# A decoder block with expert gathers: token mixers in three groups of blocks instead of two

## The chip, the cores and the metric

The kernel runs on one core of a Trainium2 chip. The metric is the device time of one execution in microseconds (us). The inputs are float32 and lie in HBM; the output goes there too. "Faster" means a lower time.

## What is computed

One layer of a decoder for 1024 tokens of width 1024. The tokens form eight blocks of 128.

```python
h = rms_norm(x, norm_mix_g)
proj = h @ w_in                    # queries, keys, values of two attentions, indexer, gates
o_a = diff_attention(...)          # 4 heads, causal, two softmaxes subtracted
o_b = dsa_attention(...)           # 8 heads, each query sees its 256 best keys by the indexer
x = x + (g[:d] * (o_a @ w_branch_a) + g[d:] * (o_b @ w_branch_b)) @ w_out
x = x + memory_attention(rms_norm(x), rms_norm(mem), w_mem_q, w_mem_kv, w_mem_o)
x = x + peer_ffn(rms_norm(x), peer_w_q, peer_sub_keys, peer_u, peer_v)
return rms_norm(x, final_norm_g)

def peer_ffn(h):                   # per token 8 heads x 16 experts of 16384
    s_top, i_top = top_k(q . sub_keys, 16)       # two lists of 16 for each head
    best, idx = top 16 of the 256 pair sums; g = softmax(best)
    a = gelu(sum(h * u[idx])) * g
    return sum(a * v[idx])
```

Attention is causal: block b looks at the keys of blocks 0 to b, so blocks can be worked in groups from the front.

## The kernel before

**Groups.** `run` (L1304) goes over `GROUPS`: blocks 0 to 3, then 4 to 7. For a group it calls `phase_P` (norm, projections with w_in, the indexer's scores), `phase_T` (the two attentions, L634), `phase_G` (gates and branch products), `phase_O` (w_out), `queries_M` and `phase_M` (memory attention), `phase_R` (scores of the expert keys, written to DRAM as `pq`). Every phase streams its weights from HBM again for each group, in 256 KB tiles two to a load (`wstream`, L165). Where `WHOLE` does not name the phase and group, ScalarE and VectorE split a tile into a rounded part and a rest (L106, L107), and a product is three matmuls (L129 to L131). Where it does, one float32 matmul is used (L127). `by_pairs` takes w_out and w_mem_o of the first group for two blocks at a time.

**Experts.** Blocks 0 to 3 get their experts by gathers. After the first group `run` adds two lanes to a pace-maker. `routes` finds the 128 experts of each token of a block (`route`: a load `so<-pq`, then lists of the 16 best on VectorE, L928 to L932). `experts` gathers the rows in the fixed order `ORDER`, U then V of block 0, of block 1, and so on: 128 gathers of u rows a block (L1036, issued by GpSimd, 512 KB each), each followed by a multiply-and-sum on VectorE (L1039), and 128 gathers of v rows (L1052), each followed by a multiply-and-add (L1058); 1024 in all. Seven buffers `rows` hold gathered rows. Blocks 4 to 7 get theirs in `dense`: all 16384 experts go through TensorE and are weighted by a sparse table, which is built on chip beside the first 48 of 128 expert tiles ("early", their gelu is kept in DRAM as `ga` and read back as `c`). The rest of the tiles follow, with the second product added up in `accu` (L1282).

**What sets the order.** Each phase tells the pace-maker how much TensorE work it has emitted (`tick`, in nominal us). A lane emits its next piece when its credit allows: a gather each `u_each` nominal us, taken from `U_EACH`. A list scheduler then fixes each engine's order, with the lanes at a lower priority (`ROUTE_LAG`, `EXPERT_LAG`). On the chip each engine works its list in order. The lane `fill` puts gate products and memory keys between the attention's small matmuls, `select` the search for the 256 best keys.

```python
self.pace.add("routes", routes, ROUTE_EACH, ROUTE_LAG)
self.pace.add("experts", self.experts(routes), None, EXPERT_LAG)
```

Of the kernel before, what the change touches and what calls it, by code (L numbers as in the profile page):

```python
# [20 lines left out]
P = 128  # L21
S = 1024
D = 1024
NB = S // P
GROUPS = [[0, 1, 2, 3], [4, 5, 6, 7]]
NG = 4
ND = NB - NG
DT = ND * P
# [50 lines left out]
class K:  # L79
# [245 lines left out]
    def phase_P(self, g, st, hp, hT):  # L325
# [3 lines left out]
        with ExitStack() as ctx:  # L329
            E = ctx.enter_context  # L330
            self.pp = pp = E(self.pool("pp"))
            self.wp = E(self.pool("wP"))
            self.scr2 = (pp, "x", "h", X_BUFS[g], D)
            gm = self.gain(pp, a["norm_mix_g"], "gmix")
            for i, b in enumerate(blks):
                x = pp.tile([P, D], F32, name="x", bufs=X_BUFS[g])
                nc.sync.dma_start(x, a["x"][0, b * P:(b + 1) * P])
                h = pp.tile([P, D], F32, name="h", bufs=X_BUFS[g])
                self.norm(h, x, gm)
# [136 lines left out]
            project([(w_in, C_DSQ, 512)], 512, use_dsq)  # L476
            self.pace.tick(START_T[g])

# [155 lines left out]
    def phase_T(self, g, oT, hT):  # L634
# [3 lines left out]
        with ExitStack() as ctx:  # L638
# [1 line left out]
            SM, NR, LD = nk * P, ROWS_T[g], LOADS_T[g]  # L640
            self.scr2 = (tp, "row", "row", NR, SM)
            if g:
                self.u_each = U_EACH[g + 1]

            for h in range(4):
                ks = tp.tile([P, 2, SM], F32R, name="k", bufs=LD)
# [544 lines left out]
    def dense(self, psum, early):  # L1191
# [5 lines left out]
        with ExitStack() as ctx:  # L1197
# [19 lines left out]
            ga = {}  # L1217
            with ExitStack() as c2:
                self.wb = c2.enter_context(self.pool("wb"))
                self.u_each = U_EACH[-2]  # L1220
                self.pace.add("weights", self.weights(blks))
                for e in range(early):
                    o = first(e)
                    t = self.wb.tile([P, 512], F32, name="gelu", bufs=2)
                    nc.scalar.activation(t, o, AF.Gelu)
                    ga[e] = self.scratch([P, 512], f"ga{e}")
                    nc.sync.dma_start(ga[e], t)
                self.pace.drain("weights")
# [3 lines left out]
            for n in range(KEEP):  # L1232
                i, d = n % ND, n // ND
                kept[i, d] = self.ps.tile([P, 512], F32, name=f"kept{n}", bufs=1)
            self.u_each = U_EACH[-1]
            sp = E(self.pool("sp"))
            accu = sp.tile([P, ND, D], F32, name="accu")
            G = 4
# [65 lines left out]
    def run(self, ctx):  # L1304
# [13 lines left out]
        self.scored = set()  # L1318
        for g, self.blks in enumerate(GROUPS):
            self.GB, self.GT = len(self.blks), len(self.blks) * P  # L1320
            if g:
                self.u_each = U_EACH[g]
            psum.close()
            with self.pool(f"hT{g}", side="right") as hp, self.pool(f"W{g}", side="right") as st, \
                    self.pool(f"fp{g}", side="right") as self.fp, self.pool(f"fill{g}", side="right", space=PSUM) as self.fps:
# [10 lines left out]
            psum = self.psum_phase(psum, f"psG{g}", 6)  # L1336
            last = g == len(GROUPS) - 1
            side = "right" if last else None
# [30 lines left out]
            if g == 0:  # L1369
                self.setup_peer(ctx.enter_context(self.pool("peer", side="right")))  # L1370
                self.route_ctx = ExitStack()
                self.setup_route(self.route_ctx.enter_context(self.pool("rt", side="right")))
                self.rs, self.routed = {b: {} for b in range(NG)}, set()
                routes = self.routes(range(NG))
                self.u_each = U_EACH[0]
                self.pace.add("routes", routes, ROUTE_EACH, ROUTE_LAG)
                self.pace.add("experts", self.experts(routes), None, EXPERT_LAG)
        self.pace.drain("routes")
# [6 lines left out]
EARLY = 48  # L1385
V_AHEAD, V_EACH = 0, None
ORDER = [("U", 0), ("V", 0), ("U", 1), ("V", 1), ("U", 2), ("V", 2), ("U", 3), ("V", 3)]
ROWS_T, LOADS_T, FILL_EACH, FILL_LAG = (5, 4), (2, 2), (0.7, 2.4), 100
H_BUFS, D_BUFS, R_BUFS = (4, 2), 4, 7
X_BUFS = (3, 1)  # L1390
START_T = (0.0, 0.0)
WHOLE = {("P", 1), ("G", 1), ("M", 1)}
PAIRS = {(2, 0)}
KEEP, A_BUFS, O_BUFS = 4, 2, 2
U_BUFS, V_BUFS = 3, (4, 4, 4)
SELECT_EACH = (5.0, 7.0)
U_EACH, ROUTE_EACH = (1.9, 1.8, 1.9, 1.3, 2.0), 3.0
ROUTE_LAG, EXPERT_LAG = 300, 3000
_INS = ["x", "mem", "positions", "norm_mix_g", "w_in", "da_lambda", "da_subln_g", "w_branch_a", "w_branch_b", "gate_bias",
        "w_out", "norm_mem_g", "mem_kv_norm_g", "w_mem_q", "w_mem_kv", "w_mem_o", "norm_ffn_g", "peer_w_q",  # L1400
# [29 lines left out]
```

## Time and profile before

| What | Value |
|---|---|
| median of 3 runs | 3506.3 us (3505.97 to 3508.13) |
| the profiled execution, its span | 3509.34 us, 3507.6 us |
| TensorE (PE) busy | 3015.4 us, 86% |
| VectorE (DVE) busy | 2878.4 us, 82% |
| ScalarE (ACT), GpSimd (POOL) busy | 1396.7 us, 1380.4 us |
| moved by DMA | 964.65 MB, 275 GB/s in the mean |
| mean granted TensorE clock | 0.928 |

The span is one execution from its first to its last instruction, on the profiler's clock; the execution's own time is 1.7 us more. Busy times are unions of an engine's instructions. They are averages over stages that differ much, so they are read stage by stage. The granted clock is a share of 2.4 GHz; TensorE runs at 2.4 or at 1.2.

### The profile page before, as it was taken

How to read it: one execution, taken by the hardware profiler on the slowest of the kernel's cores; microseconds unless marked ns; L12 is line 12 of the kernel's file. 1: busy time of each engine (PE TensorE's matmuls, PEld its weight loads, DVE VectorE, ACT ScalarE, POOL GpSimd, SP SyncE). 2: the span in 40 equal slices, each digit the busy share in tenths (PEclk: the TensorE clock that was granted, in tenths of full speed). 3: DMA queues.
4: the chain of work that ended last, by engine and by line, in shares of the span. 5: the costliest groups of instructions: out<-in, count | busy, mean ns of one | idle time of the engine just before them, and what ended most of it. 6: DMA issues, size and time to landing. Idle time of an engine off the chain costs nothing.

```text
span 3507.6 us, 42342 instructions
## 1 busy us (share of the span) xinstructions
PE 3015.4 (86%) x13234; PEld 2285.7 (65%) x13234; DVE 2878.4 (82%) x6695; ACT 1396.7 (40%) x2537; POOL 1380.4 (39%) x1122
## 2 busy tenths in 40 slices
PE   8999888798787698686989995588899999999995
PEld 7777766553355575455767774466687788777884
DVE  6656544599888879888988988687799999999998
ACT  5755344245565441322546456222222222222221
POOL 0000000011235246553131466333466665767665
PEclk9999998999898799888999998799899999999998
DMA  4575443436789579897485899999999999999997
GB/s 138 162 186 133 162 140 137 132 121 198 223 259 312 139 272 356 306 328 272 163 314 189 309 379 341 375 309 321 318 351 372 376 380 365 382 379 373 383 382 265
DMA packets 394210, 964.65 MB, mean 275 GB/s; under 512 B 36712, under 2 KB 146048, under 8 KB 392576
## 3 DMA queue, kind: packets, MB, share of 16 engines
q0 software_dynamic: 155264, 560.01, 45.0%
q1 hardware_dynamic: 238720, 401.94, 33.3%
q8 instruction: 104, 1.70, 0.2%
q14 instruction: 122, 1.00, 0.1%
HBM read 871.64 MB, written 90.18 MB: 274 GB/s over the span
## 4 chain that ended last, share of the span: by engine, by line
PE 35%; DVE 21%; DMA 17%; issue 15%; POOL 8%; ACT 4%; SPq 1%; POOLq 0%; ACTq 0%; DVEq 0%
POOL rows L1036 5%; PE acc L129 5%; PE acc L131 5%; PE acc L130 5%; DMA c<-ga 4%; DVE h3s L1058 3%; DMA rows<-in_peer_v_dram,ii 2%; DMA so<-pq 2%; PE fill L127 2%; POOL rows L1052 2%; PE po L720 2%; DVE rows L1039 2%; DMA fraw<-in_w_in_dram 1%; DMA rows<-in_peer_u_dram,ii 1%; PE tps L601 1%
## 5 line engine op out<-in xcount | busy, mean ns | idle before, releaser
L1036 POOL DMA_INDIRECT rows<-in_peer_u_dram,ii x512 | 656.8, 1283 | 917.2 <-DVE rows L1039 304.9
L1052 POOL DMA_INDIRECT rows<-in_peer_v_dram,ii x512 | 660.6, 1290 | 447.4 <-DVE h3s L1058 290.9
L1058 DVE SCALAR_TENSOR_TENSOR h3s<-rows,wexp,h3s 128x1024 f32<-128x1024 f32 x508 | 651.1, 1282 | 34.4 <-DMA rows<-in_peer_v_dram,ii 25.1
L1039 DVE SCALAR_TENSOR_TENSOR rows<-rows,h3s 128x1024 f32<-128x1024 f32 x512 | 612.0, 1220 | 62.7 <-DMA rows<-in_peer_u_dram,ii 62.2
L129 PE MATMUL acc<-fT,uT 128*128 128x512 f32 x1024 | 415.6, 406 | 38.6 <-ACT uT L106 23.2
L131 PE MATMUL acc<-fT,uT 128*128 128x512 f32 x1024 | 411.8, 402 | 15.3 <-DVE uT L107 15.2
L130 PE MATMUL acc<-fT,uT 128*128 128x512 f32 x1024 | 410.5, 401 | 0.0
L106 ACT ACTIVATE c<-wl 128x512 fp32r<-128x512 f32 x128 | 80.2, 631 | 805.6 <-PE out L130 479.2
L143 POOL TENSOR_TENSOR rstd<-msq,mhalf 128x1 f32<-128x1 f32 (+1 forms) x42 | 34.0, 808 | 596.1 <-DVE msq L141 572.5
L129 PEld LDWEIGHTS acc<-fT,uT 128*128 128x128 f32 x1024 | 196.5, 192 | 84.7 <-ACT uT L106 23.6
L131 PEld LDWEIGHTS acc<-fT,uT 128*128 128x128 f32 x1024 | 196.7, 192 | 64.4 <-DVE uT L107 23.7
L106 ACT ACTIVATE uT<-uraw 128x1024 fp32r<-128x1024 f32 x128 | 135.6, 1059 | 254.2 <-PE acc L130 131.0
L130 PE MATMUL kept<-v,c 128*128 128x512 f32 x512 | 206.2, 405 | 32.3 <-DVE v L107 32.2
L129 PE MATMUL kept<-v,c 128*128 128x512 f32 x512 | 201.4, 400 | 37.1 <-ACT v L106 35.8
L130 PEld LDWEIGHTS acc<-fT,uT 128*128 128x128 f32 x1024 | 197.0, 192 | 45.3 <-issue 6.0
L129 PE MATMUL out<-v,c 128*128 128x512 f32 x512 | 203.6, 398 | 15.2 <-DVE accu L1282 15.2
L107 DVE TENSOR_TENSOR w<-wraw,w 128x512 fp32r<-128x512 f32 (+1 forms) x176 | 116.4, 680 | 116.3 <-ACT w L106 109.5
L131 PE MATMUL kept<-v,c 128*128 128x512 f32 x512 | 203.7, 398 | 0.0
L130 PE MATMUL out<-v,c 128*128 128x512 f32 x512 | 201.9, 394 | 0.0
L131 PE MATMUL out<-v,c 128*128 128x512 f32 x512 | 201.8, 394 | 0.0
L562 ACT ACTIVATE junk<-W,xb 128x384 bf16<-128x384 f32 (+5 forms) x186 | 163.7, 880 | 78.8 <-DVE xb L560 76.1
L127 PE MATMUL acc<-wraw,hT 128*128 128x512 f32 (+1 forms) x384 | 169.3, 597 | 16.2 <-ACT tok L349 7.6
(367 smaller groups left out, 6731.6 us busy)
## 6 DMA issues: line engine op xcount, KB each, us to landing
uraw<-in_peer_ut_dram SPq DMA_DIRECT2D x128, 512.0 KB, 9.2
vraw<-in_peer_v_dram SPq DMA_DIRECT2D x128, 512.0 KB, 8.8
Wd<-wbuf SPq DMA_DIRECT2D x64, 512.0 KB, 8.6
wl<-Wd SPq DMA_DIRECT2D x64, 512.0 KB, 8.4
wraw<-in_w_in_dram SPq DMA_DIRECT2D x40, 512.0 KB, 3.6
fraw<-in_w_in_dram SPq DMA_DIRECT2D x32, 512.0 KB, 6.0
wraw<-in_w_out_dram SPq DMA_DIRECT2D x24, 512.0 KB, 4.2
ga<-gelu SPq DMA_DIRECT2D x48, 256.0 KB, 5.4
```

The source lines that it names most:

```text
L106: self.nc.scalar.activation(hi, src, AF.Copy)
L107: self.last_dve = self.nc.vector.tensor_tensor(lo, src, hi.bitcast(F32), op=OP.subtract).ins
L127: self.last_pe = nc.tensor.matmul(out, l[0], r[0], start=start, stop=stop).ins
L129: nc.tensor.matmul(out, l[0], r[0], start=start, stop=False)
L130: nc.tensor.matmul(out, l[0], r[1], start=False, stop=False)
L131: self.last_pe = nc.tensor.matmul(out, l[1], r[0], start=False, stop=stop).ins
L562: nc.scalar.activation(junk[:, :(b + 1) * P], self.W[b], AF.Sign, bias=xb[:, j:j + 1].bitcast(F32), accum_out=s[:, j:j + 1])
L720: nc.tensor.matmul(po[:, h * 64:(h + 1) * 64], pT[:, j * P:(j + 1) * P], self.dsv[:, k0 + j, gg * 64:(gg + 1) * 64], start=(k0 + j == 0), ...
L1036: nc.gpsimd.indirect_dma_start(out=u, out_offset=None, in_=a["peer_u"][0], in_offset=bass.IndirectOffsetOnAxis(ap=ii[:, j:j + 1], axis=0))
L1039: nc.vector.scalar_tensor_tensor(u, u, 1.0, h3, op0=OP.mult, op1=OP.mult, accum_out=aa[:, j:j + 1])
L1052: nc.gpsimd.indirect_dma_start(out=v, out_offset=None, in_=a["peer_v"][0], in_offset=bass.IndirectOffsetOnAxis(ap=r["ii"][:, j:j + 1], axi ...
L1058: nc.vector.scalar_tensor_tensor(o, v, w[:, j:j + 1], o, op0=OP.mult, op1=OP.add)
```

## The change

Blocks 0 to 3 are mixed in two groups of two. The lanes for routing and gathers are started after the first group, as before, so the routing of blocks 0 and 1 can begin after those two blocks, and that of 2 and 3 after the second group. The last group is as it was. The tables by group have a third entry. `phase_P` makes indexer queries only for groups that have a block of 2 or more (it did so before too), so the first group of two makes none.

```diff
-GROUPS = [[0, 1, 2, 3], [4, 5, 6, 7]]
+GROUPS = [[0, 1], [2, 3], [4, 5, 6, 7]]
...
-                self.u_each = U_EACH[g + 1]
+                self.u_each = U_EACH["T", g]
...
-                self.u_each = U_EACH[-2]
+                self.u_each = U_EACH["W"]
...
-            self.u_each = U_EACH[-1]
+            self.u_each = U_EACH["D"]
...
-                self.u_each = U_EACH[g]
+                self.u_each = U_EACH["P", g]
...
-                self.u_each = U_EACH[0]
...
-ROWS_T, LOADS_T, FILL_EACH, FILL_LAG = (5, 4), (2, 2), (0.7, 2.4), 100
-H_BUFS, D_BUFS, R_BUFS = (4, 2), 4, 7
-X_BUFS = (3, 1)
-WHOLE = {("P", 1), ("G", 1), ("M", 1)}
-PAIRS = {(2, 0)}
+ROWS_T, LOADS_T, FILL_EACH, FILL_LAG = (5, 5, 4), (2, 2, 2), (0.22, 0.7, 2.4), 100
+H_BUFS, D_BUFS, R_BUFS = (2, 2, 2), 4, 7
+X_BUFS = (2, 2, 1)
+WHOLE = {("P", 2), ("G", 2), ("M", 2)}
+PAIRS = {(2, 0), (2, 1)}
...
-SELECT_EACH = (5.0, 7.0)
-U_EACH, ROUTE_EACH = (1.9, 1.8, 1.9, 1.3, 2.0), 3.0
+SELECT_EACH = (0.0, 2.5, 7.0)
+U_EACH = {("P", 1): 1.9, ("T", 1): 1.9, ("P", 2): 1.8, ("T", 2): 1.9, "W": 1.3, "D": 2.0}
+ROUTE_EACH = 3.0
```

The intervals of the gathers are the same numbers as before at the stages that were there before: 1.9 beside the mixers, 1.3 in the early experts, 2.0 in the dense ones.

**Where gathers now stand on GpSimd (POOL).** `L1036` and `L1052` are the gathers of u and v rows, `L616` and `L648` the loads of queries and keys for an attention head, `L143` a norm's root, `L907` the set-up of routing. Before, from there to the second head of the second group:

```order
L907 IOTA place 128x50
L143 TENSOR_TENSOR rstd<-msq,mhalf 128x1 x4
L1036 DMA rows<-in_peer_u_dram,ii 128x1024 x40
L616 DMA q<-daq_7439 64x4x512 x2
L648 DMA k<-dak 128x2x1024
```

In the change, from there to the third head of the second group, which now holds blocks 2 and 3:

```order
L907 IOTA place 128x50
L143 TENSOR_TENSOR rstd<-msq,mhalf 128x1 x6
L1036 DMA rows<-in_peer_u_dram,ii 128x1024 x3
L616 DMA q<-daq_4755 64x4x256 x2
L648 DMA k<-dak 128x2x512
L616 DMA q<-daq_4755 64x4x256 x2
L648 DMA k<-dak 128x2x512
L1036 DMA rows<-in_peer_u_dram,ii 128x1024
L616 DMA q<-daq_4755 64x4x256 x2
L648 DMA k<-dak 128x2x512
L1036 DMA rows<-in_peer_u_dram,ii 128x1024 x6
```

And on the same engine from that group's last attention head to the third group's first work there (`L553`, the set-up of its selection):

```order
L143 TENSOR_TENSOR rstd<-msq,mhalf 128x2
L1036 DMA rows<-in_peer_u_dram,ii 128x1024 x61
L143 TENSOR_TENSOR rstd<-msq,mhalf 128x1 x2
L1036 DMA rows<-in_peer_u_dram,ii 128x1024 x33
L143 TENSOR_TENSOR rstd<-msq,mhalf 128x1 x2
L1036 DMA rows<-in_peer_u_dram,ii 128x1024 x12
L553 IOTA flip 128x4
```

So 116 gathers (3, 1, 6, 61, 33 and 12) stand between the end of the first group and the third; none stood before the group of blocks 4 to 7.

**At the start of the early experts**, on POOL too; `L1103` is the first instruction of `make_codes`. Before:

```order
L143 TENSOR_TENSOR rstd<-msq,mhalf 128x1
L1036 DMA rows<-in_peer_u_dram,ii 128x1024
L143 TENSOR_TENSOR rstd<-msq,mhalf 128x1
L1036 DMA rows<-in_peer_u_dram,ii 128x1024 x35
L1103 IOTA ah 112x128
```

In the change:

```order
L1036 DMA rows<-in_peer_u_dram,ii 128x1024 x33
L1052 DMA rows<-in_peer_v_dram,ii 128x1024
L143 TENSOR_TENSOR rstd<-msq,mhalf 128x1 x4
L1052 DMA rows<-in_peer_v_dram,ii 128x1024 x29
L1103 IOTA ah 112x128
```

Added up from the start, 297 gathers stand ahead of it before (u of blocks 0 and 41 of block 1, v of block 0) and 414 in the change (u and v of block 0, u and 30 v of block 1).

**The last gathers on VectorE (DVE)**, among the accumulations `L1282`; `L1071` and `L148` are a block's last sum and norm. Before, the end of the program:

```order
L141 TENSOR_SCALAR msq<-ss 128x1
L1058 SCALAR_TENSOR_TENSOR h3s<-rows,wexp,h3s 128x1024 x2
L148 SCALAR_TENSOR_TENSOR uraw<-uraw,rstd,vraw 128x1024
L1058 SCALAR_TENSOR_TENSOR h3s<-rows,wexp,h3s 128x1024 x5
L1071 TENSOR_TENSOR rows<-rows,h3s 128x1024
```

In the change 20 of the 124 accumulations stand behind these rows:

```order
L107 TENSOR_TENSOR uT_29095<-uraw,uT_29094 128x1024
L1058 SCALAR_TENSOR_TENSOR h3s<-rows,wexp,h3s 128x1024
L1071 TENSOR_TENSOR rows<-rows,h3s 128x1024
L1282 TENSOR_TENSOR accu<-accu,out 128x512
L141 TENSOR_SCALAR msq<-ss 128x1
L148 SCALAR_TENSOR_TENSOR rows<-rows,rstd 128x1024
```

The last gather moved from the end of the program to a place with several groups of expert tiles behind it. In VectorE's order 481 gathers are used before the first accumulation before, 580 in the change.

## Rows read from the trace of the kernel before

**Rows 1.** Windows by stage: stretch, its length, busy us (instructions), granted clock, DMA share, GB/s.

```profile
core 0: us, PE busy (x) PEld busy (x) DVE busy (x) ACT busy (x) POOL busy (x), PEclk, DMA share, GB/s
0.00:653.00 653.00, 582.94 (x2758) 463.68 (x2758) 347.53 (x964) 331.02 (x754) 28.39 (x51) 0.95 0.51 150
653.00:1635.00 982.00, 775.45 (x2980) 491.49 (x2980) 858.81 (x2752) 426.10 (x957) 390.76 (x338) 0.88 0.74 249
1635.00:2214.00 579.00, 495.31 (x2552) 388.28 (x2552) 514.70 (x1557) 308.61 (x392) 222.21 (x172) 0.94 0.77 283
2214.00:2520.00 306.00, 235.04 (x922) 184.04 (x923) 231.00 (x295) 67.45 (x89) 109.28 (x91) 0.88 0.94 326
2520.00:3471.00 951.00, 926.68 (x4023) 758.21 (x4022) 904.17 (x1110) 260.11 (x339) 619.47 (x464) 0.99 0.99 369
3471.00:3508.00 37.00, 0.00 (x0) 0.00 (x0) 22.17 (x21) 3.45 (x6) 10.27 (x8) 0.54 0.59 199
```

**Rows 2.** Chain of waits (start, us, what): first work of two stages.

```profile
653.09 6.64 DMA x<-in_x_dram
...
1634.79 2.29 DVE codes L1114
```

**Rows 3.** Windows: the last part of the first group.

```profile
410.00:653.00 243.00, 203.86 (x824) 155.58 (x822) 102.24 (x207) 93.76 (x180) 5.06 (x11) 0.90 0.43 143
```

**Rows 4.** Groups of DVE by form, 0 to 653 us: busy us, mean ns, idle before.

```profile
L107 DVE TENSOR_TENSOR w<-wraw,w 128x512 fp32r<-128x512 f32 x128 | 85.5, 689 | 110.5 <-ACT w L106 104.1 <-PE acc L130 6.2
L107 DVE TENSOR_TENSOR f<-fraw,f 128x512 fp32r<-128x512 f32 x48 | 33.0, 688 | 37.4 <-ACT f L106 30.9 <-PE tps L355 5.1 <-PE fill L131 0.8
```

**Rows 5.** Groups of DVE by form, 650 to 1640 us: gathers, lists of 16, pair match.

```profile
L1039 DVE SCALAR_TENSOR_TENSOR rows<-rows,h3s 128x1024 f32<-128x1024 f32 x164 | 198.1, 1219 | 17.7 <-DMA rows<-in_peer_u_dram,ii 17.5
L1058 DVE SCALAR_TENSOR_TENSOR h3s<-rows,wexp,h3s 128x1024 f32<-128x1024 f32 x127 | 162.8, 1282 | 8.9 <-DMA rows<-in_peer_v_dram,ii 6.0
...
L929 DVE FIND_INDEX8 i<-v,so 128x8 uint32<-128x128 f32 x79 | 22.3, 284 | 0.0
L932 DVE FIND_INDEX8 i<-v,t 128x8 uint32<-128x128 f32 x76 | 21.5, 284 | 0.0
L931 DVE MAX8 v<-t 128x8 f32<-128x128 f32 x77 | 21.2, 282 | 0.1
L930 DVE MATCH_REPLACE8 t<-v,so 128x128 f32<-128x128 f32 x77 | 21.1, 275 | 0.0
L928 DVE MAX8 v<-so 128x8 f32<-128x128 f32 x79 | 20.7, 281 | 45.1 <-DMA so<-pq 45.1
...
L995 DVE TENSOR_TENSOR eq<-eq,kn 128x512 f32<-128x512 f32 x16 | 10.9, 680 | 0.0
```

**Rows 6.** Timeline of PE: 256-column matmuls of split products (start, length).

```profile
311.54 0.28 PE L131 MATMUL fill<-memT,f 128*128 128x256 f32 x1
311.66 0.28 PE L129 MATMUL fill<-memT,f 128*128 128x256 f32 x1
```

**Rows 7.** Windows: the dense stage beside u gathers (first) and v gathers (second).

```profile
2600.00:2700.00 100.00, 95.45 (x410) 77.24 (x409) 93.38 (x146) 26.78 (x35) 68.35 (x50) 0.98 1.00 376
2750.00:2950.00 200.00, 200.00 (x884) 165.62 (x883) 197.41 (x191) 54.02 (x70) 134.91 (x100) 1.00 1.01 379
```

**Rows 8.** The tile `ga`: its reloads (first and last start), who waited (us, times).

```profile
L1249 SPq DMA_DIRECT2D c<-ga x48: 319/323/5063, 2214.3 to 2537.2; - x48
...
DVE wl L1253: 54.0, 31
```

**Rows 9.** The tile `so`: who waited for it, and its DMAs' time to landing.

```profile
DVE v L928: 55.5, 9
...
DMA to landing us min/median/max: 2.0/3.3/16.0
```

**Rows 10.** Windows: 50 us of the second group with little TensorE work.

```profile
1150.00:1200.00 50.00, 22.20 (x128) 20.01 (x129) 46.87 (x117) 14.94 (x50) 7.74 (x8) 0.63 0.26 83
```

**Rows 11.** Timeline of DVE: the end.

```profile
3492.75 6.56 DVE L1058 SCALAR_TENSOR_TENSOR h3s<-rows,wexp,h3s 128x1024 f32<-128x1024 f32 x5
```

More of the change, by code (lines that the diff above doesn't have):

```diff
@@ L1387 @@
 ORDER = [("U", 0), ("V", 0), ("U", 1), ("V", 1), ("U", 2), ("V", 2), ("U", 3), ("V", 3)]
-ROWS_T, LOADS_T, FILL_EACH, FILL_LAG = (5, 4), (2, 2), (0.7, 2.4), 100
-H_BUFS, D_BUFS, R_BUFS = (4, 2), 4, 7
-X_BUFS = (3, 1)
-START_T = (0.0, 0.0)
-WHOLE = {("P", 1), ("G", 1), ("M", 1)}
-PAIRS = {(2, 0)}
+ROWS_T, LOADS_T, FILL_EACH, FILL_LAG = (5, 5, 4), (2, 2, 2), (0.22, 0.7, 2.4), 100
+H_BUFS, D_BUFS, R_BUFS = (2, 2, 2), 4, 7
+X_BUFS = (2, 2, 1)
+START_T = (0.0, 0.0, 0.0)
+WHOLE = {("P", 2), ("G", 2), ("M", 2)}
+PAIRS = {(2, 0), (2, 1)}
 KEEP, A_BUFS, O_BUFS = 4, 2, 2
 U_BUFS, V_BUFS = 3, (4, 4, 4)
-SELECT_EACH = (5.0, 7.0)
-U_EACH, ROUTE_EACH = (1.9, 1.8, 1.9, 1.3, 2.0), 3.0
+SELECT_EACH = (0.0, 2.5, 7.0)
+U_EACH = {("P", 1): 1.9, ("T", 1): 1.9, ("P", 2): 1.8, ("T", 2): 1.9, "W": 1.3, "D": 2.0}
+ROUTE_EACH = 3.0
 ROUTE_LAG, EXPERT_LAG = 300, 3000
```

## Prediction

> **What bounds the kernel now.** I read the windows by stage first, cut where the chain of waits and the first reload of a gelu tile show the next stage's first work [rows 1, 2, 8]: the first group 0 to 653 us, the second 653 to 1635, the early experts 1635 to 2214, the dense experts 2214 to 3471, and 37 us of final norms without a matmul. The reader should see a different limit in each.
> The first group is TensorE's: busy 583 of 653 us, while VectorE works 348 and no gather runs. Its 70 idle us fall unevenly: 39 of them lie in its last 243 us, where the output projection, memory attention and routing scores start one after another [rows 1, 3]. The second group is VectorE's: 859 of 982 us, 87%, TensorE 775. The early stage is both (515 and 495 of 579). In the dense stage after 2520 TensorE is busy 927 of 951, with VectorE at 904 and DMA at 0.99. Before 2520 it is idle 71 of 306; there VectorE waits 54 us for the reload of 48 gelu tiles, which no gather causes [rows 8].
> So 1024 gathers, each 1.2 to 1.3 us of VectorE [rows 5], start late, and VectorE idles 305 us in the first group. That is the room the change goes for.
>
> **The change, part by part.** Stages are compared with the profiled execution (3509.3 us for a span of 3507.6; the median of the runs is 3 us lower).
>
> *Matmul count.* Where the group's tokens are the moving side, a 512-column matmul becomes two of 256. By the built program's counts 288 such matmuls become 576 for each of the three products of a split multiply: 864 pairs. Undisturbed 256-column matmuls start 0.12 us apart [rows 6], 512-column ones 200/884 = 0.226 [rows 7]; a pair costs 0.24 for 0.226, some 10 us in all. Against it stand 48 matmuls (11 us) of indexer queries that blocks 0 and 1 do not need and no longer make. TensorE's work is unchanged: about 291 us for each small group.
> The Trainium skill says otherwise in TensorE: Matmul & The Clock Gate, section Back-to-back issue gap: sustained spacing is set by weight load and matmul together, 81 ns at 128 columns and 131 at 512. A straight line between them is 98 ns at 256 by estimate, so a pair would cost 65 ns more than one, 56 us over the 864. This trace shows another spacing for these split fp32 products, at both widths, and the sum goes by the trace.
>
> *First group, now blocks 0 and 1.* 291 us of matmuls, plus 4 for half of the pairs' cost, less 11. The 39 us of starts come once per group whatever its size, because each is a norm, a transpose and a first weight load in series. Of the other 31 idle us I count 22, between half and all. Sum 345. Its bounds: 323 (no idle time but the starts) and 370 (weights twice as fast per matmul and late). VectorE is no limit: 144 weight splits at 0.69 us [rows 4] and half of the rest come to 210.
>
> *Second group, blocks 2 and 3.* New here is that VectorE gets everything at once. Splits: 136 of 0.69 us and 8 narrower ones at two thirds, 98 us, since each group splits every weight again. The rest of the first group's VectorE work is 348 - 119 = 229 us [rows 1, 4]; blocks 2 and 3 carry all indexing and selection, so 120. Routing of blocks 0 and 1: a list of the 16 best costs 1.41 us over five rows and a block has 16 such lists, 23 us; the pair match has twelve steps of 0.68 a block, another 8 [rows 5], the many short steps about 14 by estimate: 45 a block, 90. Gathers: the order puts 116 before the third group's first POOL work, 140 us at 1.21. Sum 448 against 291 of TensorE. At the 87% of the present second group this takes 512 us; at 95% 472, at 80%, which 256 KB weight tiles going DMA, ScalarE, VectorE, TensorE in turn may bring, 560. I take 512, since the same mixture ran at 87%. The two small groups together: 857, or 204 more than the 653 now.
> TensorE's granted clock is a cost that hides here: where it was busy 22 of 50 us the clock was 0.63 in the mean, a mixture of 2.4 and 1.2 GHz [rows 10]. Even at 0.8 its 291 us become 364, below VectorE's 448.
>
> *Third group, the old second.* Two routings fewer (90 us of VectorE), 298 gathers for 297. VectorE 770; at 87% that is 880, a gain of 102. With TensorE at 775 of work the stage cannot follow VectorE all the way down: none to 102, and I take 70, two thirds, since VectorE's share there is 87% and TensorE's 79%. Eight loads of scores fewer, at up to 16 us each [rows 9], are inside this.
>
> *Early experts.* 166 gathers for 184, same interval 1.3: 23 us of VectorE between two engines equally busy. 0 to 26; I take 10.
>
> *Dense experts.* 444 gathers are left at the first accumulation instead of 543 (in VectorE's order). The interval stays 2.0, so they end sooner, 20 accumulations of 124 before the end. What does a removed gather return? While value rows are gathered TensorE runs 884 matmuls in 200 us and is never idle: nothing to return. While u rows are gathered it runs 410 in 100 us where the other rate is 442, 7% fewer, at 50 gathers [rows 7]: 0.15 us a gather, 10 us over the 68 u gathers fewer. With 4 for the value rows: 14. Bounds: 0, and TensorE's whole idle time from 2214 to 3471, 306 - 235 + 951 - 927 = 95.
>
> *End.* The last five gathers run 3492.8 to 3499.3 and the fourth block's norm behind them [rows 11]. After the change only the dense blocks' norms stand there: 12 us less, 0 to 20.
>
> *DMA.* 52 loads of 512 KB more, 27 MB, are hidden: the first group moves 150 GB/s at a busy share of 0.51, and the dense stage shows 369 GB/s [rows 1]. If that cover goes, at 369 GB/s they cost 74 us, mostly in the two small groups; that is in the upper bounds.
>
> Sum: +204 - 70 - 10 - 14 - 12 = +98. 3509.3 + 98 - 3 = 3604, given as **3605**.
>
> **The rivals.**
> *A, faster: the dense stage belongs to VectorE, not TensorE.* Then each gather taken out returns its 1.28 us divided by 0.95, up to the 95 us idle; the third group returns its full 102, the early stage 26, the end 20. Total -243 against +204: 3467. It decides if more than four fifths of those returns come. For it: VectorE at 93 and 99% in the dense windows, DMA at 1.0 [rows 7]. Against: TensorE idle 0 of 200 us beside 100 gathers [rows 7], and the 54 us wait for gelu tiles that stays [rows 8]. Chance 0.12.
> *B, much slower: the second group's VectorE queue stands behind the loads of scores.* Each list waits for a load into a single buffer; VectorE lost 55 us to it in nine waits, and a load lands in 3.3 us in the median, 16.0 at worst [rows 9]. In the second group they now run beside doubled weight traffic and gathers, and what is queued behind them is the split of the next weight tile, so TensorE waits too. Eight loads at 16.0 instead of 3.3 are 100 us: 3705. It decides if loads land beyond 10 us. Chance 0.14.
> *C, the gathers do not follow their group.* The order shows that they do so late: three stand on POOL before the second group's first attention load, ten before its last head's. Those 116 do run before the third group in any case, so this moves cost within the second group and gives no other time; it is in the forecast.
>
> **How the numbers follow.** The forecast has 0.74. Its terms reach from 472 to 560 in the second group (-40, +48), -22 and +25 in the first, -32 and +70 in the third, -12 and +24 in the dense stage and the end. Below, I add the ends straight, since all four fall together if VectorE can be kept fuller: 3605 - 106 = 3499. Above, in quadrature, +92: 3697. The range is 3500 to 3695; it leaves out A and about half of B, 0.19. A measurement of this kernel tells about 0.2%, 7 us, from no change. Faster: A and 0.01 from the forecast's lower edge, 0.13. Same: 0.04. Slower: 0.83.
>
> **What the profile would show.** Right: the third group starts near 857, with VectorE at 85 to 90% in the stretch before it and TensorE's clock below 0.9 there; codes L1114 near 1770; the dense stretch within 30 us of its old 1257, its last part without gathers at 222 matmuls in 50 us as before. Wrong: a third group that starts before 800 (VectorE can hold more than 87%), or after 930 (B, with waits of VectorE for score loads); a dense stage shorter by more than 60 us (A). Wrong too if the first group is over 380 at unchanged TensorE work: then weights, not matmuls, set its pace.

## The result and the profile after

The changed kernel takes 3719.1 us in the median of four runs (3702.75 to 3726.61), the kernel before 3507.2 (3505.97 to 3508.2): a ratio of 1.0598, 95% interval 1.0561 to 1.0635. It is 212 us slower; 98 were forecast, and the time lies above the range.

The windows by stage of the changed kernel, cut at the same events as [rows 1]: first load of `x` of a group, `codes`, first reload of a gelu tile, last matmul. The two first lines stand for the first line of [rows 1], the dense stage is one line.

```profile
core 0: us, PE busy (x) PEld busy (x) DVE busy (x) ACT busy (x) POOL busy (x), PEclk, DMA share, GB/s
0.00:373.00 373.00, 300.89 (x1764) 262.54 (x1764) 209.50 (x574) 178.87 (x404) 20.86 (x39) 0.90 0.63 189
373.00:892.00 519.00, 343.49 (x1826) 287.25 (x1826) 422.07 (x1412) 223.70 (x516) 161.60 (x146) 0.81 0.74 242
892.00:1887.00 995.00, 779.26 (x2980) 496.24 (x2980) 772.48 (x2096) 427.94 (x957) 395.17 (x337) 0.88 0.71 243
1887.00:2448.00 561.00, 489.85 (x2552) 383.19 (x2552) 499.07 (x1500) 308.39 (x392) 181.43 (x154) 0.94 0.76 280
2448.00:3704.00 1256.00, 1164.46 (x4944) 947.25 (x4944) 1040.42 (x1272) 329.14 (x430) 608.28 (x462) 0.96 0.88 321
3704.00:3714.00 10.00, 0.13 (x1) 0.00 (x0) 3.77 (x5) 1.15 (x2) 0.55 (x1) 0.67 0.30 122
```

Against [rows 1] the small groups take 892 us for 653 (+239), the third group 995 for 982 (+13), the early experts 561 for 579 (-18), the dense ones 1256 for 1257, the tail 10 for 37 (-27): +206 in all, the difference of the two spans (3714.0 and 3507.6). Two things stand out. In the third group VectorE has 86 us less to do and TensorE the same, and the group is not shorter: VectorE's share falls from 87 to 78%. And TensorE is busy 644 us in the small groups for 583 before, at a granted clock of 0.90 and 0.81 for 0.95; the prediction had foreseen a clock below 0.9 for the second group, as a cost that hides, and took no lower clock for the first.

Who waited for the tile `so` in the changed kernel, the routing's loads of scores, as in [rows 9], with their time to landing:

```profile
  DVE v L928: 33.8, 10
...
DMA to landing us min/median/max: 2.0/5.5/8.8
```

VectorE waits less for them than before (33.8 us for 55.5), and none lands later than 8.8 us: rival B's mechanism is not what made the time longer, though its 3705 is near it. The reload of the gelu tiles, as in [rows 8], is nearly as it was (48.0 us for 54.0):

```profile
  DVE wl L1253: 48.0, 26
```

### The profile page after: what moved, and what is told of

The parts are those of the page before. It is cut to its first block, busy times and chain, and to the rows that moved or that the text cites. A ratio compares the mean times of both kernels' runs of the same rounds, so it can differ in the third digit from the quotient of the medians.

```text
span 3714.0 us, 44631 instructions
## 1 busy us (share of the span) xinstructions
PE 3078.1 (83%) x14066; PEld 2376.5 (64%) x14066; DVE 2947.3 (79%) x6855; ACT 1469.2 (40%) x2701; POOL 1367.9 (37%) x1138
## 2 busy tenths in 40 slices
DMA packets 424606, 998.66 MB, mean 269 GB/s; under 512 B 39576, under 2 KB 172464, under 8 KB 422832
## 5 line engine op out<-in xcount | busy, mean ns | idle before, releaser
L1052 POOL DMA_INDIRECT rows<-in_peer_v_dram,ii x512 | 653.1, 1276 | 757.5 <-DVE h3s L1058 429.0
L1036 POOL DMA_INDIRECT rows<-in_peer_u_dram,ii x512 | 644.5, 1259 | 738.1 <-DVE rows L1039 417.7
L129 PE MATMUL acc<-fT,uT 128*128 128x512 f32 x1024 | 413.6, 404 | 38.3 <-ACT uT L106 26.1
L143 POOL TENSOR_TENSOR rstd<-msq,mhalf 128x1 f32<-128x1 f32 (+2 forms) x46 | 33.5, 728 | 671.0 <-DVE msq L141 642.3
L129 PEld LDWEIGHTS acc<-fT,uT 128*128 128x128 f32 x1024 | 196.0, 191 | 82.1 <-ACT uT L106 26.9
L129 PE MATMUL kept<-v,c 128*128 128x512 f32 x512 | 203.4, 403 | 45.2 <-ACT v L106 44.2
L107 DVE TENSOR_TENSOR w<-wraw,w 128x512 fp32r<-128x512 f32 (+1 forms) x256 | 167.5, 676 | 80.3 <-ACT w L106 79.7
L106 ACT ACTIVATE w<-wraw 128x512 fp32r<-128x512 f32 (+1 forms) x256 | 151.9, 617 | 197.2 <-PE acc L130 58.1
L129 PE MATMUL out<-v,c 128*128 128x512 f32 x512 | 205.0, 400 | 10.1 <-DVE accu L1282 10.0
```

The costliest lines, as they stand in the source:

```text
L106: self.nc.scalar.activation(hi, src, AF.Copy)
L107: self.last_dve = self.nc.vector.tensor_tensor(lo, src, hi.bitcast(F32), op=OP.subtract).ins
L129: nc.tensor.matmul(out, l[0], r[0], start=start, stop=False)
L143: nc.gpsimd.tensor_tensor(r, v, self.mhalf[:, :n], op=OP.pow)
L1036: nc.gpsimd.indirect_dma_start(out=u, out_offset=None, in_=a["peer_u"][0], in_offset=bass.IndirectOffsetOnAxis(ap=ii[:, j:j + 1], axis=0))
L1052: nc.gpsimd.indirect_dma_start(out=v, out_offset=None, in_=a["peer_v"][0], in_offset=bass.IndirectOffsetOnAxis(ap=r["ii"][:, j:j + 1], axi ...
```

## The experiments

All take the kernel before or the changed one as base. Stage lengths are read at the events named above: small groups | third group | early | dense | tail. They are of one profiled execution. The times are medians of 4 to 12 executions where the text gives a ratio, of one otherwise; the kernel before, run beside the experiments, had medians of 3502 to 3514 us.

| kernel | stages, us | time, us |
|---|---|---|
| before | 653 (one group) \| 982 \| 579 \| 1257 \| 37 | 3507 |
| changed | 373 + 519 \| 995 \| 561 \| 1256 \| 10 | 3719 |
| third group with 26 gathers | 375 + 522 \| 870 \| 570 \| 1267 \| 278 | 3885 |
| second group with 15 gathers | 375 + 446 \| 971 \| 583 \| 1270 \| 41 | 3687 |
| routing after the second group | 375 + 404 \| 987 \| 579 \| 1269 \| 34 | 3640 |
| that, deeper weight buffers | 365 + 405 \| 977 \| 577 \| 1262 \| 33 | 3619 |
| before, routing of two blocks twice | 651 \| 1077 | 3605 |
| before, gathers earlier | 651 \| 1080 \| 562 \| 1258 \| 10 | 3566 |
| changed, a quarter of VectorE's columns | 376 + 502 \| 935 \| 589 \| 1230 \| 12 | 3646 |
| changed, a quarter of the loads | 378 + 469 \| 930 \| 528 \| 1199 \| 9 | 3516 |
| before, a quarter of the loads | 655 \| 941 \| 550 \| 1180 \| 20 | 3348 |
| routing after the second group, a quarter of the loads | 377 + 406 \| 1000 \| 549 \| 1182 \| 20 | 3536 |

### What the gathers cost in each small stage

**e1**, the changed kernel with next to no gathers in the third group (26 are left).

```diff
-("P", 2): 1.8, ("T", 2): 1.9
+("P", 2): 30.0, ("T", 2): 30.0
```

> The change with an interval of 30 nominal us for gathers in the third group's projections and attention (1.8 and 1.9 in the change); the order leaves 26 gathers in the third group where the change has 298. Read the third group alone, from its first load of x to the codes: 995 us in the change. Theory V (VectorE sets this stage, as predicted): 272 gathers are 340 us of VectorE, so the stage falls to TensorE's work, about 830 us. Theory T (TensorE's own chains and its lower clock set it, gathers cost only where they crowd the DMA queues): about 940 to 960. The whole gets slower in both, since some 890 gathers are left for the experts' stages, which hold about 730; 3850 to 4000.

The third group takes 870 us, 125 less for 272 gathers fewer, 0.46 us each, between what the two theories expected (830, 940 to 960). The time is 3885 us, since the kernel then runs 278 us past the last matmul to use up its gathers. So a gather costs far less in a mixer group than VectorE's 1.25 us, but it isn't free there.

**e2**, the same for the second small group (15 gathers are left).

```diff
-("P", 1): 1.9, ("T", 1): 1.9
+("P", 1): 30.0, ("T", 1): 30.0
```

> The change with an interval of 30 for gathers in the second group; the order leaves 15 gathers there for 116. Read the second group: 519 us in the change. Theory V (VectorE's sum sets it): 101 gathers fewer are 122 us of VectorE, at 82% about 150 us: 370 to 400. Theory T (a group of two is a chain of starts, whatever runs beside): 470 to 500. The dense stage then holds gathers to its end and gets the tail of the kernel before (37 for 10 us).

The second group takes 446 us for 519, again between the two theories (370 to 400, 470 to 500): 101 gathers cost 73 us, 0.72 each. The time is 3687 us. In sum neither engine fills the second group: VectorE is busy 309 of its 446 us here, TensorE 332 at a clock of 0.83.

```profile
375.00:821.00 446.00, 331.67 (x1826) 279.76 (x1826) 309.29 (x1203) 223.98 (x516) 33.14 (x43) 0.83 0.54 163
```

**e3**, lanes started after the second group, so the split stands almost alone.

```diff
-            if g == 0:
+            if g == 1:
```

> The change with routing and gathers started after the second group instead of the first, so that the two small groups run bare, and the third has all four routings as the kernel before. It splits the 239 us that the two small groups cost over the old first group (653) into the price of the split itself and that of what was put beside it. Theory V: the split costs about 100 (373 and 375 us), sharing 140. Theory T: the split alone costs 150 or more (373 and 430). The third group: V 1050 or more, as 90 us of routing come back; T 980 to 1000. The whole: V 3600 to 3620, T 3640 to 3680.

The time is 3640 us, a ratio of 1.0381 to before (1.0355 to 1.0406); the two small groups take 779 us. The split itself costs 126 us of the 239. (49 of the 96 routing lists of blocks 0 to 3 run between 625 and 779 us, in the second small group's last part, which at 174 us is 8 longer than the first group's 166: they cost little there. So only half of the routing came back to the third group, and its 987 us are no test of the 1050 that theory V expected.) The second group of e2 has nearly the same number, 48, but 40 of them before 550 us, beside projections and attention. VectorE has nearly the same work there (309 us for 300), and the group takes 446 us for 404 here: the place of the lists, with 15 gathers, makes 42 us. The second group of e3:

```profile
375.00:779.00 404.00, 316.66 (x1826) 274.53 (x1826) 299.57 (x1155) 223.66 (x517) 16.75 (x27) 0.88 0.53 161
```

Windows of the phases: projections, attentions, and everything from the gates to the scores. First the one group before:

```profile
0.00:213.00 213.00, 191.09 (x898) 153.81 (x899) 124.28 (x404) 132.20 (x289) 10.58 (x22) 1.00 0.58 161
213.00:384.00 171.00, 161.98 (x925) 132.77 (x924) 102.51 (x324) 97.14 (x272) 12.74 (x18) 0.96 0.56 148
384.00:653.00 269.00, 229.86 (x939) 177.10 (x937) 120.73 (x237) 101.67 (x194) 5.06 (x11) 0.91 0.43 143
```

Then the two groups of e3:

```profile
0.00:102.00 102.00, 76.50 (x393) 64.18 (x394) 61.96 (x174) 50.46 (x92) 9.51 (x20) 0.96 0.79 234
102.00:209.00 107.00, 96.12 (x648) 85.65 (x648) 58.47 (x180) 59.11 (x174) 8.94 (x14) 0.95 0.69 181
209.00:375.00 166.00, 126.79 (x727) 110.28 (x725) 78.31 (x160) 66.75 (x136) 2.42 (x6) 0.85 0.45 158
375.00:495.00 120.00, 97.80 (x518) 82.31 (x518) 80.22 (x226) 85.88 (x195) 5.07 (x8) 0.93 0.66 190
495.00:605.00 110.00, 88.48 (x585) 79.30 (x586) 69.71 (x231) 71.89 (x190) 9.46 (x15) 0.90 0.47 122
605.00:779.00 174.00, 130.38 (x725) 112.93 (x723) 149.64 (x699) 65.89 (x134) 2.22 (x4) 0.82 0.48 165
```

The last phase is idle on TensorE for 39 us before (269 - 230), and for 39 and 44 us in the two groups: the idle time comes once per group, whatever its size, as forecast. But so it does in the other phases: 31 us before, 36 and 44 in the two groups. In sum TensorE's idle time goes from 70 to 163 us (+93), its busy time from 583 to 616 (+33) at a lower granted clock.

### Is the idle time late weights?

**e5**, e3 with more buffers for weights.

```diff
-        self.abufs, self.wraw = 6, 3
+        self.abufs, self.wraw = 6, 5
...
-                raw = self.wp.tile([P, 2, 512], F32, name="wraw", bufs=2)
+                raw = self.wp.tile([P, 2, 512], F32, name="wraw", bufs=4)
...
-            raw = fp.tile([P, 2 * per, width], F32, name="fraw", bufs=2)
+            raw = fp.tile([P, 2 * per, width], F32, name="fraw", bufs=4)
```

> The kernel of the third experiment (small groups bare) with deeper buffers for weight tiles: five for three in the streams, four for two where two blocks are taken at a time and in the fill between attention's matmuls. Read the two small groups: 779 us there, 653 for the same blocks in one group. Theory W (a weight tile serves half the matmuls, so it comes late): 745 or less. Theory S (each group has its own series of norms, softmaxes and first loads, and TensorE at its lower clock in them): 765 to 785.

The small groups take 365 + 405 for 375 + 404: 9 us of 126. Late loads are a small part. **e9** does the second of these edits alone in the kernel before, as a candidate for a faster one:

> The kernel before with four buffers instead of two for the weight pairs of w_out and w_mem_o in the first group. Theory S (the starts are chains of norm, transpose, split and first matmul; the load is not late): 3500 to 3508, no change that can be measured. Theory W (weights of these products land late): 10 us and more faster, taken out of the stretch 384 to 653, so 3497 or less.

3502.9 us for 3501.9, a ratio of 1.0005 (0.9993 to 1.0017): no change. What TensorE waits for in the stretch 0 to 779 us (line, waited for: us, times, longest), in the kernel before, where the stretch holds the whole first group and 126 us of the next:

```profile
PE tps L156 <- DVE h L148: 24.5, 5, 14.1
PE acc L129 <- ACT w L106: 13.8, 5, 9.6
...
PE fill L129 <- ACT f L106: 3.4, 2, 3.1
```

and in e3:

```profile
PE tps L156 <- DVE msq L141: 32.3, 6, 16.0
PE acc L129 <- ACT w L106: 31.9, 7, 6.9
PE fill L129 <- ACT f L106: 20.1, 5, 10.2
PE tps L848 <- DVE rm L845: 12.8, 6, 2.5
```

The longest are transposes behind a norm (L156) and the first product behind a weight's rounding (L129); both are more in e3. These are chains through ScalarE and VectorE at a phase's start, and each group has its own.

### Are narrow matmuls dear?

**e12**, the kernel before with 820 matmuls of the first group cut in two (the first of each accumulation stays whole).

```diff
-        nc.tensor.matmul(out, l[0], r[1], start=False, stop=False)
...
+            for c in cuts:
+                self.last_pe = nc.tensor.matmul(out[:, c:c + m], x, y[:, c:c + m], start=False,
+                                                stop=last and c == cuts[-1]).ins
```

> The kernel before, in two groups, with 820 of the first group's 512-column matmuls that take weights as the stationary side issued as two of 256 columns each; loads, splits and starts stay. If a pair costs 0.24 us for 0.226 (spacing read from the trace): +11 us, 3513 to 3520. If a pair costs 65 ns more than one matmul (the rule of the Trainium skill, TensorE: Matmul & The Clock Gate, Back-to-back issue gap): +53, about 3555. If a pair costs what both matmuls show as busy time in the first group (0.30 us for a 256-column one beside 0.40 for 512), the stretch 0 to 653 grows by up to 160 and the time to 3660.

3518.6 us, a ratio of 1.0030 (1.0013 to 1.0046), +5 to +16 us. The first group ends at 664.4 us:

```profile
0.00:664.40 664.40, 588.98 (x3578) 509.79 (x3578) 349.19 (x967) 332.52 (x754) 28.49 (x51) 0.96 0.50 148
```

That is 11.3 us more for 820 pairs, 13.8 ns a pair; 14 were read from the spacing in [rows 6] and [rows 7]. Columns are not what the split costs.

### Is VectorE the bound of the big mixer group?

**e8**, the kernel before with the routing of blocks 2 and 3 made twice (some 90 us more for VectorE).

```diff
-        for _ in self.route(b, r):
-            yield
+        for _ in range(2 if b >= 2 else 1):
+            for _ in self.route(b, r):
+                yield
```

> The kernel before with the routing of blocks 2 and 3 made twice: 90 us more of VectorE's work in the second group, the size of the step that the prediction counted with 70 us in the change's third group. Theory V: second group 982 to 1050, whole 3570 to 3590. Theory T (routing falls into VectorE's gaps there; what costs is a gather, 0.42 us): 982 to 995, whole 3505 to 3525.

3605 us, a ratio of 1.0258 (1.0228 to 1.0288); the group takes 1077 us, more than either theory expected (up to 1050). In the second group of this kernel VectorE has 86 us more to do:

```profile
651.00:1728.00 1077.00, 770.15 (x2980) 485.90 (x2980) 944.69 (x3321) 428.88 (x960) 398.00 (x339) 0.85 0.67 230
```

**e7**, the kernel before with the gathers pulled forward: 363 used before `codes` for 292.

```diff
-U_EACH, ROUTE_EACH = (1.9, 1.8, 1.9, 1.3, 2.0), 3.0
+U_EACH, ROUTE_EACH = (1.5, 1.5, 1.5, 1.2, 1.9), 3.0
```

> The kernel before, two groups, with shorter intervals everywhere (1.5 for 1.9, 1.8 and 1.9 beside the mixers, 1.2 for 1.3 in the early experts, 1.9 for 2.0 in the dense ones): the order uses 71 gathers more before the codes and ends them 12 accumulations before the last. It is the change's second half without its first: gathers moved out of the dense stage without splitting a group. Theory T: the second group pays 0.42 us for each, +30; the dense stage returns nothing, the tail 25: 3500 to 3515. Theory V: the dense stage returns 1.28 us for each, 3440 to 3470.

3566 us, a ratio of 1.0147 (1.0117 to 1.0178), which neither theory expected (3500 to 3515, 3440 to 3470); the group grew by 98 us, far more than the 0.46 us per gather that e1 suggests:

```profile
651.00:1731.00 1080.00, 771.52 (x2980) 487.24 (x2980) 941.44 (x2891) 426.83 (x957) 475.70 (x409) 0.85 0.76 260
```

Both follow one line: VectorE is busy 945 of 1077 us and 941 of 1080, 88 and 87%, as it was 859 of 982 in [rows 1]. With more for VectorE to do, the group grows by that divided by 0.87. The other way it does not go: with 772 the changed kernel's third group takes 995 us (78%), with 786 that of e3 takes 987 (80%), with 752 that of e2 takes 971 (77%). The third groups of e3 and e2:

```profile
779.00:1766.00 987.00, 782.95 (x2980) 496.71 (x2980) 785.81 (x2208) 427.91 (x957) 408.76 (x339) 0.88 0.72 247
821.00:1792.00 971.00, 777.79 (x2980) 493.75 (x2980) 751.79 (x2086) 427.89 (x955) 365.13 (x320) 0.89 0.70 239
```

So with two routings fewer the group returned next to nothing. Whether VectorE stops being the bound right below what it had before is not shown by this alone: in all three kernels the group also starts with more gathers, 88 to 95 in its first phase for 40 in the kernel before (see below), which may take what less routing gives.

### What takes its place: VectorE's columns or the loads of gathered rows

**e10** and **e11**, the changed kernel with a quarter of VectorE's columns for each gathered row, or with a quarter of each load. Both leave out part of what the experts of blocks 0 to 3 give.

```diff
-nc.vector.scalar_tensor_tensor(u, u, 1.0, h3, op0=OP.mult, op1=OP.mult, accum_out=aa[:, j:j + 1])
+nc.vector.scalar_tensor_tensor(u[:, :256], u[:, :256], 1.0, h3[:, :256], op0=OP.mult, op1=OP.mult, accum_out=aa[:, j:j + 1])
...
```

```diff
-nc.gpsimd.indirect_dma_start(out=u, out_offset=None, in_=a["peer_u"][0],
+nc.gpsimd.indirect_dma_start(out=u[:, :256], out_offset=None, in_=a["peer_u"][0].rearrange("e (a c) -> (e a) c", a=4),
...
```

> The changed kernel; VectorE multiplies only 256 of the 1024 columns of each gathered row (three quarters of the products of the experts of blocks 0 to 3 are left out), while every row is still gathered whole at the same place. Theory V (VectorE's time for the gathers sets the second and the third group): a gather there takes about 0.4 instead of 1.25 us, so the second group falls from 519 to about 446 (that of the kernel with bare second group) and the third from 995 to about 880, the span to 3525. Theory Q (what counts is the transfer, or the place of the gathers in GpSimd's queue): the second group stays over 500, the third over 970, the span over 3680. Dense experts within 20 us of 1256 in both.

> The changed kernel; each gather moves only the 256 columns of a quarter row (128 KB for 512, wrong rows, so what the experts of blocks 0 to 3 give is left out), at the same place in GpSimd's queue; VectorE still works 1024 columns of each value row and 768 of each u row. Theory V (VectorE's time sets the second and third group): second group 490 to 519, third 965 to 995, span over 3650. Theory D (the transfers of the gathers crowd out weights and score loads): second group about 446, third about 880, span about 3530. If both this kernel and the one with a quarter of VectorE's work stay where the changed kernel is, it is neither, and the order of the queues is left.

Second and third group of e10:

```profile
376.00:878.00 502.00, 356.03 (x1826) 298.45 (x1826) 339.59 (x1426) 223.34 (x516) 144.31 (x154) 0.80 0.77 254
878.00:1813.00 935.00, 762.90 (x2980) 484.55 (x2980) 553.70 (x2083) 429.90 (x957) 307.47 (x328) 0.89 0.74 256
```

and of e11, with its dense stage:

```profile
378.00:847.00 469.00, 337.96 (x1826) 283.37 (x1826) 393.83 (x1413) 223.27 (x516) 160.67 (x148) 0.81 0.58 171
847.00:1777.00 930.00, 766.59 (x2980) 492.75 (x2980) 736.12 (x2095) 428.76 (x957) 375.21 (x334) 0.90 0.45 133
...
2305.00:3504.00 1199.00, 1147.39 (x4944) 938.48 (x4944) 981.48 (x1262) 329.47 (x430) 581.49 (x458) 0.97 0.56 183
```

Neither theory holds alone. In the second group VectorE loses 82 us of work in e10 and the group only 17; the smaller loads, with 28 us less of VectorE's work, return 50. In the third group each returns 60 to 65, and to the same place: 935 and 930 (e11 with 36 us less of VectorE's work). Together that is as much as taking nearly all of its gathers out returned (e1, 125). So columns and loads seem to make about half each of what a gather costs there, though VectorE is busy 78% only; no run has both changes. In the early and dense stages the loads count: e11 takes 528 and 1199 us for 561 and 1256. VectorE's columns do not. e10 takes 589 and 1230 us (a dense stage within 20 us of 1256 was expected), with 38 gathers more in the early stage and 38 fewer in the dense one, so 1819 for 1817 together, though VectorE has 472 us less to do there:

```profile
1813.00:2402.00 589.00, 501.60 (x2552) 383.90 (x2552) 395.29 (x1574) 302.39 (x392) 191.67 (x192) 0.94 0.81 307
2402.00:3632.00 1230.00, 1157.69 (x4944) 943.35 (x4944) 672.63 (x1194) 326.80 (x427) 434.65 (x423) 0.97 0.85 308
```

The reload stretch shows what the loads do, by the first and last start of the 48 reloads; in the changed kernel

```profile
L1249 SPq DMA_DIRECT2D c<-ga x48: 319/326/2654, 2447.8 to 2778.5; - x48
```

and in e11, with VectorE's wait for them:

```profile
L1249 SPq DMA_DIRECT2D c<-ga x48: 319/326/587, 2305.0 to 2578.3; - x48
...
  DVE wl L1253: 21.0, 16
```

331 us became 273: all of the 57 us that the dense stage lost. VectorE's wait fell from 48.0 to 21.0 us, so the gathers' loads cause a part of it.

**e13** and **e14** are the kernel before and e3 with the same quarter loads.

> The kernel before with gathers of 128 KB instead of 512 KB, as in the changed kernel with quarter loads (what the experts of blocks 0 to 3 give is left out). Stages before: 653, 982, 579, 1257, 37. Theory D1 (the transfers cost the changed kernel and the one before alike): second stage 982 to about 915, early to 550, dense to 1200, span about 3340, so the changed kernel stays some 170 behind at quarter loads (3514). Theory D2 (they cost the changed kernel alone, since its gathers run ahead into stages that load weights): the kernel before falls by less than 60, to 3450 or more.

> The split kernel that routes and gathers only after its second small group, with gathers of 128 KB instead of 512 KB (same part left out). Its stages with whole loads: 375, 404, 987, 579, 1269, 35. Against the kernel before with quarter loads this is the split alone. If the split's price (+126 with whole loads) is none of the gathers', it stays within 20 us of +126 in the two small groups and the rest of the two kernels agrees within 30. If the third group owes its length to transfers, it falls to 915 or less.

The kernel before falls by 161 us to 3348, so it pays for transfers too (theory D1): its early and dense stages take 106 us less, and the wait for the gelu tiles falls from 54.0 to 28.9 us; the distance between the two kernels shrinks from 212 to 168. Most of the 44 is the second small group, 519 to 469. In the third group 65 us go in the changed kernel and 41 in the kernel before, whose VectorE stays on its line (812 of 941 us, 86%): by that line its 47 us less of VectorE's work would return 54 alone, so the loads' share there is not shown. The split alone costs 127 us in the small groups of e14 against e13 (782 for 655.5), as with whole loads: its price is none of the gathers'. The third group of e14 did not shrink; it takes 1000 us for 941 in e13, 59 more where at most 30 were expected, so e14 is 188 us slower in all. Third groups by phase, first the kernel before:

```profile
653.00:958.00 305.00, 247.09 (x700) 124.61 (x700) 272.21 (x1406) 149.21 (x291) 50.18 (x50) 0.92 0.53 172
958.00:1307.00 349.00, 278.98 (x1436) 200.77 (x1436) 299.51 (x873) 197.95 (x512) 149.43 (x130) 0.88 0.77 241
1307.00:1635.00 328.00, 249.38 (x844) 166.10 (x844) 287.09 (x475) 78.94 (x154) 191.15 (x159) 0.84 0.89 329
```

the changed kernel:

```profile
892.00:1232.00 340.00, 274.33 (x765) 136.60 (x765) 280.10 (x910) 159.37 (x305) 134.26 (x113) 0.92 0.73 253
1232.00:1571.00 339.00, 258.59 (x1372) 195.22 (x1372) 262.59 (x707) 188.73 (x498) 113.23 (x106) 0.87 0.66 206
1571.00:1887.00 316.00, 246.34 (x844) 164.42 (x844) 229.79 (x479) 79.83 (x154) 147.68 (x119) 0.86 0.75 271
```

and the first phase of e14:

```profile
782.00:1147.00 365.00, 280.62 (x762) 139.57 (x762) 294.06 (x1149) 161.06 (x311) 168.41 (x144) 0.87 0.46 136
```

The later phases got shorter by 10 and 12 us, the first longer by 35. Counted in the trace from the group's first load of `x` to its first query load on GpSimd (L616), 40 gathers are issued in the kernel before and 95 in the changed one. The first phase mostly goes with that number. From the load of `x` to the first score matmul of the attention (L663) it takes 313 us with 40, 312 with 46 (e13), 343 with 95, 351 with 91 (e3), 368 with 131 (e14). But it is 317 in e11, with 105, and 335 in e10, with 100. So it is not the number alone, and how far it is GpSimd's queue, VectorE's or the loads stays open: gathers were not moved by themselves within the group.

### Does the dense stage return anything?

**e4**, the kernel before with an interval of 1.85 for 2.0 in the dense stage, and **e6**, the changed kernel with 2.8.

```diff
-U_EACH, ROUTE_EACH = (1.9, 1.8, 1.9, 1.3, 2.0), 3.0
+U_EACH, ROUTE_EACH = (1.9, 1.8, 1.9, 1.3, 1.85), 3.0
```

```diff
-"D": 2.0}
+"D": 2.8}
```

> The kernel before with gathers in the dense stage each 1.85 nominal us for 2.0, so that they end before the last matmul, as they do in the change. The change's tail behind the last matmul is 10 us, that of the kernel before 37. If the crowd in the dense stage costs nothing (the change: 99 gathers fewer there, stage 1256 us for 1257): 3480 to 3490. If each dense us that gets a denser crowd is paid by TensorE: 3500 to 3520.

> The change with gathers in the dense stage each 2.8 nominal us for 2.0: the same 444, spread over the whole stage instead of ending 20 accumulations before its end. Read the dense stage, 1256 us in the change. Theory T (beside TensorE's matmuls a gather is free as long as it fits): 1245 to 1260, tail 20 to 37 for 10, whole 3705 to 3745. Theory V (the crowd sets the pace): a thinner crowd gives 1215 or less.

e4 took 3518 us (1.0031, 1.0012 to 1.0051): VectorE's order had the last gather at the last accumulation as before, so it made nothing denser and tells nothing. In e6 the stage took 1243 us for 1256, and the gathers then ended 61 us after the last matmul: 3760 us, above the 3705 to 3745 expected. Spreading them over the stage returns 13 us at most. e7 tells more: with 501 gathers used by VectorE in its dense stage for 549 in the kernel before, the stage took 1258 us for 1257.

## Why the prediction was wrong

The sign and the place of most of the cost were right; the size was not. Of the 108 us that are missing in the sum, 28 are the first group's, 7 the second's and 83 the third's; the rest gives back 10. By the terms of the sum:

- **Matmul count, +10: right.** e12 measured +11.3 for 820 pairs. The -11 for matmuls that fall away was not measured by itself. By the prediction's estimate from the Trainium skill, TensorE: Matmul & The Clock Gate, section Back-to-back issue gap, which it weighed and set aside, the 820 pairs would have cost 53; the measurement agrees with the trace.
- **First group, 345: 373.** The 39 us of starts per group are there (39 and 44 in e3). Two things were mis-sized: the other idle time (22 taken, 36 measured in e3, for 31 in a group twice as large) and TensorE's busy time (284 taken, 300 measured, at 0.90 for 0.95).
- **The clock "hides": unsaid where it mattered, not shown where it was said.** In the first group VectorE is busy 210 of 373 us and covers nothing. In the second VectorE's work is not the bound (next point), so nothing shows that TensorE's 343 us at 0.81 hid behind it; what the clock alone cost there no run tells.
- **Second group, 512: 519, for the wrong reason.** VectorE's work was foreseen (448; 422 measured), but it is not the bound: without 82 us of it the group takes 502 (e10), and its share was 81%, not the 85 to 90 foretold. The 519 are 404 with the lists in the last phase (e3), 42 for the lists beside projections and attention with 15 gathers (e2), and 73 for 101 more gathers.
- **Third group, -70: +13. This is the step that failed most, 83 of the 108 us.** It took VectorE's 87% as a rule that holds in both directions, and two thirds of what it gives. e7 and e8 show it upward. Downward it did not hold: e2, e3 and the changed kernel stay at 971 to 995 us at 77 to 80%. In the changed kernel a quarter of the columns and a quarter of the loads return 60 and 65 us (e10, e11), so both still count there, and no share of one engine prices the relief. The group's first phase also became longer, with 55 more gathers in it. How much of the missing 83 is this crowd and how much a bound that stands right behind VectorE stays open. That two routings are some 90 us of VectorE's work was right: e8 added 86.
- **Early -10: -18. Dense -14: -1. Tail -12: -27.** Small, and they nearly cancel. The dense stage returned nothing for 85 gathers fewer (464 for 549 on VectorE); the 0.15 us for one beside u rows did not come. The stretch of the reloads, where TensorE is idle most, has as many gathers as before (101 issued for 95). That no gather causes the wait for the gelu tiles there was a wrong reading: e11 and e13 cut it to about half. The part without gathers runs at 222 matmuls in 50 us, as foretold:

```profile
3550.00:3600.00 50.00, 50.00 (x222) 41.42 (x221) 23.24 (x26) 16.21 (x20) 0.00 (x0) 1.00 0.41 134
```

- **DMA "hidden": not so for the gathers.** The prediction looked at the 52 loads of weights (27 MB; 34 MB more were moved in all, 998.66 for 964.65) and not at the gathers' own 512 KB, moved into a stage that loads weights. Quarter loads take 50 us from the second group and 65 from the third, with 28 and 36 us less of VectorE's work. What the weights' loads alone cost no run separates; deeper buffers gave back 9 us (e5).
- **Rival A** falls: the dense stage did not move by 2 us. **Rival C** gave no time of its own, since it only moves cost within the second group. The place mattered: nearly the same number of lists cost 42 us more beside projections and attention than in the last phase (e2 with its 15 gathers, e3).

The forecast's marks told it: `codes` came at 1887 for 1770 and the third group at 892 for 857, a first group of 373 stood just inside its mark of 380. No version here that computes the whole layer beats the kernel before.

## What to carry to other kernels

Halving a group of rows halves the work of its phases but not their idle time: here TensorE's idle time was 70 us for the whole group and 76 and 87 us for its halves, and a TensorE with more gaps got a lower clock on top. A share of a busy engine ("VectorE at 87%") priced added work here (e7, e8), but not removed work: first look for what stands next, and for what moves into the place that is freed, since here the length stayed. Work that moves into idle time of one engine brings its transfers along: price them in the stage that they arrive in.

## What was not expected of the hardware

- The granted clock of TensorE fell with the gaps: from 0.91 to 0.85 and 0.82 in the last phase of the small groups, where it was busy 230 of 269 us before and 127 of 166 and 130 of 174 in e3. The share alone does not give the clock: the first phase of e3 had 0.96 at 76 busy of 102 us. The kernel with more, narrower matmuls and hardly more idle time (e12, 75 us for 70) held 0.96.
- Rows gathered at 128 KB for 512 KB (with a quarter less of VectorE's columns for u rows) took 161 us from the kernel before and 204 from the changed one, in each stage that has gathers; only the third group of e14 did not get shorter (1000 us for 987 in e3). Beside them the 48 gelu tiles were reloaded in 273 us for 331, though TensorE's and VectorE's work there was nearly the same (239 and 240 us for 254 and 248).
